# Mamba2 decay matrices from cumulated decays spread through a DRAM scratch, and the residual scaling in the HGRN stage

## The chip, the cores and the metric

One core of one Trainium2 chip runs the whole program in one launch. The time is device time in microseconds, the median of several runs. Its engines are TensorE (PE, with its weight loads PEld), VectorE (DVE), ScalarE (ACT), GpSimd (POOL) and SyncE (SP, which issues the weight loads). Each runs its own instruction list in order and waits for the others by semaphores.

## The reference

Two transformer-like blocks on 512 tokens of width 1024, in float32. The second puts 16 learned tokens in front (528 in all) and feeds two mixers from one projection: HGRN2 (8 heads) and Mamba2 (16 heads in 2 groups), whose outputs are projected back together and added to the residual. The part that matters here, cut from the Mamba2 mixer:

```python
da = dt * a                                   # a < 0: one decay per token and head
a_cum = jnp.cumsum(ac, axis=2)                # within a chunk
seg = a_cum[:, :, :, None] - a_cum[:, :, None, :]
l_mat = jnp.exp(jnp.where(causal[:, :, None, None], seg, -jnp.inf))
cb = jnp.einsum('bnigs,bnjgs->bnijg', cc, bc)
y_diag = jnp.einsum('bnijgh,bnjghp->bnighp', cb[..., None] * l_mat, xc)
# per chunk: y_off from the state, state = chunk decay * state + u
```

The residual that enters block 2 is block 1's output, normalised and scaled: each token's row is multiplied by one factor.

## The kernel before

Activations lie feature by token. Every large product is a `gemm`: for each of 8 k-tiles the weight is split into a rounded high part `wh` (ACT, line 82) and a rest `wl` (DVE, line 83), and three passes (`pass3`) add `XH*wh`, `XL*wh` and `XH*wl` into PSUM tiles `acc`. In block 2 the 528 tokens make two segments of 264, so one k-tile is six products. The weights of a gemm are split two gemms ahead.

All smaller work hangs between the k-tiles. A `Lane` holds generators; each `tick` after a k-tile counts a lane down, and each `yield n` asks for n ticks. This fixes where PE's small products stand among the projection products; the other engines' lists are put in order by the framework that records the program, which can bring a later instruction ahead of an earlier one on an engine.

Block 2's first stage projects the Mamba2 inputs. `m2_conv` makes each 128-feature tile: DVE scales `acc` by `R` into `mu`, ACT starts the convolution `mc`, DVE adds three taps, ACT makes the tanh into `mu`, DVE the last step; `to_tokens` transposes `mc` on PE into `xtm` (token by feature). `m2_tables` computes `dt`, `da` and, on PE with the triangle `le`, the cumulated decays and totals.

`m2_core` runs once per group, over five chunks: the 16 learned tokens and four of 128. For a chunk it needs, per head, the decay matrix. Before, that is made thus (lines 850 to 882): POOL multiplies the triangle `le` by `da`, split in a high and a low part, into tiles `sr` of 128 by 4 heads by 128; PE multiplies these by the strict triangle `gtr`, which sums the decays between two tokens into PSUM; ACT takes the exponential into `Lm`; DVE multiplies by the masked scores `cbm`; PE multiplies with `xdt`. Beside it PE makes the state's products (`S` with `mC`, `xde` with `btm`), DVE updates `S` and `yt`, and POOL multiplies `xtm` by the skip weight and adds `yt`. `prepare(c + 1)` runs during chunk c. Group 0's chunks stand among the last Mamba2 input projections, group 1's among those of the gate `z`.

`resid` multiplies the eight tiles of `H` by the token factor `R1`. Before, it is added to lane 2 as the decay tables begin, one multiply per six ticks. The HGRN stage (`hg_head`, `hg_back`, `gate`) follows, and only then `w_out` adds to `H`.

Of the kernel before, what the change touches and what calls it, by code (L numbers as in the profile page):

```python
# [126 lines left out]
class Builder:  # L127
    def __init__(self, ctx, tc, ins, out):
        self.tc, self.nc, self.ins, self.out = tc, tc.nc, ins, out
        nc = self.nc  # L130
        self.const = ctx.enter_context(tc.tile_pool(reuse_waits="tile", name="const", bufs=1))
        self.wraw = ctx.enter_context(tc.tile_pool(reuse_waits="tile", name="wraw", bufs=2))
        self.whl = ctx.enter_context(tc.tile_pool(reuse_waits="tile", name="whl", bufs=3))
        self.stat = ctx.enter_context(tc.tile_pool(reuse_waits="tile", name="stat", bufs=1))
        self.acc_p = ctx.enter_context(tc.tile_pool(reuse_waits="tile", name="accp", bufs=4, space=PSUM))
        self.sm_p = ctx.enter_context(tc.tile_pool(reuse_waits="tile", name="smp", bufs=4, space=PSUM))
        self.W = WStream(nc, ins["wts"], self.wraw, self.whl)
        self.lanes = [Lane() for _ in range(3)]
        self.hold = False
        self.pend = []  # L140

# [162 lines left out]
    def setup(self):  # L304
        nc, c = self.nc, self.const
        self.H = c.tile([P, KD, L], F32, name="H")
        self.XH = c.tile([P, KD, L], F32R, name="XH")
        self.XL = c.tile([P, KD, L], F32R, name="XL")
        self.par_t = c.tile([P, NPAR], F32, name="par_t")
        cm = c.tile([P, 4 * P + 16], F32, name="cm")  # L310
        self.four = cm[:, 4 * P:]
        self.ident, self.le, self.gt, self.ones = (cm[:, i * P:(i + 1) * P] for i in range(4))
        nc.scalar.preload_act_table_set("exp_and_others")
        nc.sync.dma_start(out=self.H[:, 0, META:L], in_=self.ins["xT"][:, 0])
        nc.scalar.dma_start(out=self.par_t[:, 0:8], in_=self.ins["par"][:, 0:8])
        self.W.load_to(0)
        for k in range(1, KD):
            nc.sync.dma_start(out=self.H[:, k, META:L], in_=self.ins["xT"][:, k])
            if k == 2:
                self.W.load_to(1)  # L320
        nc.gpsimd.dma_start(out=self.par_t[:, 8:NPAR], in_=self.ins["par"][:, 8:NPAR])
        nc.gpsimd.dma_start(out=cm, in_=self.ins["cm"])
        nc.gpsimd.dma_start(out=self.H[:, :, 0:META], in_=self.ins["metaT"])
# [434 lines left out]
    def m2_tables(self, mp, dtp):  # L758
# [31 lines left out]
        self.ts(a, a, -1.0, ALU.mult)  # L790
        self.da = w("da")
        self.mul(self.da, self.dt, bc(a))
        self.dah, self.dal = (mp.tile([P, 5, 16], F32R, name=f"da{i}") for i in "hl")
        self.gtr = mp.tile([P, P], F32R, name="gtr")
        nc.scalar.copy(self.gtr, self.gt)
        self.split(self.dah, self.dal, self.da)
        yield 12
        ps = self.sm()
        self.mm(ps[:, 16:80], self.le, self.da[:, 1:5, :])
# [5 lines left out]
        self.ei, self.cd, self.dte = w("ei"), w("cd"), w("dte")  # L805
        self.act(f2(self.ei), cum, AF.Exp)
        self.act(f2(self.cd), tot, AF.Exp)
        nc.vector.tensor_copy(f2(v), cum)
        self.sub(f2(self.dte), tot, f2(v))
        self.act(self.dte, self.dte, AF.Exp)  # L810
        self.mul(self.dte, self.dte, self.dt)
        yield 2

    def m2_conv(self, mp, accs, segs, R, j):
# [24 lines left out]
    def m2_core(self, mp, g, C, btm, cbm, xtm):  # L839
# [6 lines left out]
        def prepare(c):  # L846
            n = dims[c][0]
            x = xtm[0:n, c, 512 * g:512 * g + 512]
            b64 = lambda t: t[0:n, c, hs].unsqueeze(2).to_broadcast([n, 8, 64])
            srs, xde = [], None  # L850
            for hh in range(2):
                h0 = 8 * g + 4 * hh
                sr = []
                for i, da in enumerate((self.dah, self.dal)):
                    t = mp.tile([P, 4, P], F32R, tag=f"sr{i}", name="sr", bufs=2)
                    da = da[0:n, c, h0:h0 + 4].bitcast(F32).unsqueeze(2).to_broadcast([n, 4, n])
                    nc.gpsimd.tensor_tensor(out=t[0:n, :, 0:n], in1=da, op=ALU.mult,
                                            in0=self.le[0:n, 0:n].unsqueeze(1).to_broadcast([n, 4, n]))
                    sr.append(t)
                srs.append(sr)  # L860
            xdt = mp.tile([P, 512], F32, tag="xdt", name="xdt", bufs=2)
            self.mul(h3(xdt[0:n]), h3(x), b64(self.dt))
            if c < 4:
                xde = mp.tile([P, 512], F32, tag="xde", name="xde", bufs=1)
                self.mul(h3(xde[0:n]), h3(x), b64(self.dte))
            return srs, xdt, xde
        nxt = prepare(0)
        yield 4
        for c in range(5):
            n, tok = dims[c]  # L870
            srs, xdt, xde = nxt
            x = xtm[0:n, c, 512 * g:512 * g + 512]
            b64 = lambda t: t[0:n, c, hs].unsqueeze(2).to_broadcast([n, 8, 64])
            Ls = []
            for hh in range(2):
                ps = self.sm()
                p3 = ps[:, 0:4 * n].rearrange("p (h i) -> p h i", i=n)
                for i, t in enumerate(srs[hh]):
                    self.mm(p3[0:n], self.gtr[0:n, 0:n], t[0:n, :, 0:n], start=i == 0, stop=i == 1)
                Lm = mp.tile([P, 4, P], F32, tag="Lm", name="Lm", bufs=2)  # L880
                self.act(Lm[0:n, :, 0:n], p3[0:n], AF.Exp)
                Ls.append(Lm)
            if c:
                po = self.sm()
                self.mm(po[0:n], C[:, tok], S)
# [3 lines left out]
            md = self.par("m2d", 8 * g, 8)[0:n].unsqueeze(2).to_broadcast([n, 8, 64])  # L889
            nc.gpsimd.tensor_tensor(out=h3(x), in0=h3(x), in1=md, op=ALU.mult)  # L890
            yield 2
            for hh in range(2):
                self.mul(Ls[hh][0:n, :, 0:n], Ls[hh][0:n, :, 0:n], cbm[0:n, c, 0:n].unsqueeze(1).to_broadcast([n, 4, n]))
            if c:
                t = mp.tile([P, 512], F32, tag="yt", name="yt", bufs=1)
                self.mul(h3(t[0:n]), h3(po[0:n]), b64(self.ei))
# [7 lines left out]
            yield 5  # L904
            pd = self.sm()
            for h in range(8):
                self.mm(pd[0:n, 64 * h:64 * h + 64], Ls[h // 4][0:n, h % 4, 0:n], xdt[0:n, 64 * h:64 * h + 64])
            yield 1
            if c == 0:
                self.add(x, pd[0:n], x)  # L910
# [153 lines left out]
    def block2(self, sqh, sqg):  # L1064
        nc, tc, st = self.nc, self.tc, self.stat
        H, XH, XL = self.H, self.XH, self.XL
        W2 = T + 2
        R, R1 = self.r_tile(), self.r_tile()

        def norm2():  # L1070
            s1 = self.tok_sums(self.blocks(sqh))
            s2 = self.tok_sums(self.blocks(sqg))
            x, y, t = (st.tile([P, 8], F32, name="q" + i) for i in "xyt")
            r1, r3 = y[:, 0:4], y[:, 4:8]

            self.ts(x[:, 0:4], s1[:, 0:4], 1.0 / D, ALU.mult, EPS, ALU.add)
            self.ts(t[:, 0:4], x[:, 0:4], EPS, ALU.mult)
            self.stt(x[:, 4:8], s2[:, 0:4], 1.0 / D, t[:, 0:4], ALU.mult, ALU.add)
            self.rsqrt(x, y, t)
            yield 6  # L1080
            self.spread([r3[:, b:b + 1] for b in range(4)], R, META)
            nc.vector.tensor_copy(R[:, 0:META], self.rmeta)
            self.spread([r1[:, b:b + 1] for b in range(4)], R1, META)

        def resid():
            for k in range(KD):
                self.mul(H[:, k, META:L], H[:, k, META:L], R1[:, META:L])
                yield 6
# [6 lines left out]
        with ExitStack() as sy:  # L1095
# [26 lines left out]
            with tc.tile_pool(reuse_waits="tile", name="m2", bufs=1) as mp:  # L1122
                xtm = mp.tile([P, 5, D], F32, name="xtm")
                nc.gpsimd.memset(xtm[:, 0, :], 0.0)
                Cs = [mp.tile([P, L], F32, name=f"mC{g}") for g in range(2)]
                btms = [mp.tile([P, 5, P], F32, name=f"btm{g}") for g in range(2)]
                cbms = [mp.tile([P, 5, P], F32, name=f"cbm{g}") for g in range(2)]
                self.core_done = [False, False]
# [45 lines left out]
                proj_bc(0)  # L1174
                dtp = mp.tile([P, L + 3], F32, tag="mu", name="dtp", bufs=2)[:, 0:L]
                self.gemm16(wdt, self.par("norm1", 0, KD), segs, 4, lambda a: self.ev_r(dtp, a, segs, R))
                self.lanes[2].add(resid())
                self.lanes[0].add(self.m2_tables(mp, dtp))
                for j in range(4):
                    proj_x(j)  # L1180
# [84 lines left out]
            with tc.tile_pool(reuse_waits="tile", name="hp", bufs=1) as hp:  # L1265
# [31 lines left out]
                for h in range(8):  # L1297
                    if h:
# [14 lines left out]
                    if h > 1:  # L1313
                        gate(h - 1)
                gate(7)
                sqa = st.tile([P, L], F32, tag="sqa", name="sqa", bufs=2)

                def ev_o(m):
# [87 lines left out]
def np_consts():  # L1406
    i = np.arange(P)
    ident = np.eye(P)
    le = (i[:, None] <= i[None, :])
    gt = (i[:, None] > i[None, :])  # L1410
    cm = np.concatenate([ident, le, gt, np.ones((P, P)), i[:, None] % 32 == i[:16]], 1).astype(np.float32)
    dist = P + i[:, None] - np.arange(256)[None, :]
    dist = np.where((dist >= 0) & (dist < P), dist, 1e30).astype(np.float32)
    r64 = np.broadcast_to((np.arange(T) % 64 != 0), (P, T)).astype(np.float32)
# [10 lines left out]
def host_inputs(a, rec):  # L1425
# [41 lines left out]


IN_SHAPES = {
    "xT": (P, KD, T), "metaT": (P, KD, META), "par": (P, NPAR), "cm": (P, 4 * P + 16), "dist": (P, 256),  # L1470
    "r64": (P, T), "r32": (P, PADL), "r4": (P, 17), "wal": (P, T), "wts": (NCH, P, 1024), "wga": (P, KD, 32), "wdt": (P, KD, 32),
}

# [22 lines left out]
```

## Time and profile before

| | |
|---|---|
| median of 3 runs (lowest to highest) | 1801.13 us (1800.87 to 1802.17) |
| the profiled execution's own time | 1800.79 us |
| its span in the trace | 1799.0 us |
| PE, PEld, DVE, ACT, POOL busy | 98%, 86%, 62%, 39%, 10% of the span |
| mean granted clock of TensorE | 0.993 |
| DMA, mean | 85 GB/s |

A busy share counts instructions that run, whatever their speed: a product at the lower clock is busy for longer. PEclk in the windows shows it, 1.00 being 2.4 GHz. Matmul records overlap, so the price of a product is read from the distance of two starts. A releaser in brackets is the instruction whose end let a waiting engine go on.

### The profile page before, as it was taken

Reading aid. Unit: us, or ns where it says so; the run is one execution under the profiler, and the core shown is the slowest. Engines: PE = TensorE matmul, PEld = TensorE weight load, DVE = VectorE, ACT = ScalarE, POOL = GpSimd, SP = SyncE. Lnnn points to the kernel's source line nnn. Section 1 sums busy time; section 2 is a strip of 40 time slices with the busy share of each in tenths; the row PEclk is TensorE's granted clock in tenths of the full one; section 3 lists DMA queues with packets and bytes.
Section 4 is the critical chain, followed back from the end, with each engine's and each line's share of the span. In section 5 each row is a group of like instructions: output and inputs, shape, how many; then the busy total and the mean of one; then the engine's idle time right before and its main releaser. Section 6 shows DMA issues by size and latency. Waiting matters only on the chain. (4 is left out here: it accounts for less than half of the span.)

```text
span 1799.0 us, 26982 instructions
## 1 busy us (share of the span) xinstructions
PE 1767.2 (98%) x11036; PEld 1550.6 (86%) x11036; DVE 1116.0 (62%) x1942; ACT 703.6 (39%) x1097; POOL 174.6 (10%) x226
## 2 busy tenths in 40 slices
PE   8999999999999999999998999999999999999997
PEld 6777778888888888888887989999999999999775
DVE  5476764444467777633698798676743577776332
ACT  5355442222344444333442335545432344444221
POOL 2000000000110000011135451000001000000000
PEclk9999999999999999999998999999999999999998
DMA  5222223333333333333221212222223332333321
GB/s 183 83 71 59 71 82 94 94 94 94 94 94 94 94 94 94 94 94 95 85 71 36 60 48 80 69 82 61 83 74 92 94 88 90 94 94 94 94 84 68
DMA packets 43452, 153.50 MB, mean 85 GB/s; under 512 B 5024, under 2 KB 5168, under 8 KB 43328
## 3 DMA queue, kind: packets, MB, share of 16 engines
q1 hardware_dynamic: 42480, 149.83, 27.4%
q8 instruction: 87, 1.43, 0.3%
q0 software_dynamic: 560, 1.67, 0.3%
q14 instruction: 37, 0.30, 0.1%
q10 hardware_dynamic: 288, 0.27, 0.0%
HBM read 149.66 MB, written 2.10 MB: 84 GB/s over the span
## 5 line engine op out<-in xcount | busy, mean ns | idle before, releaser
L179 PE MATMUL acc<-XH,wh 128*128 128x512 f32 (+3 forms) x2320 | 635.5, 328 | 0.0
L179 PE MATMUL acc<-XH,wl 128*128 128x512 f32 (+3 forms) x2320 | 621.2, 321 | 0.0
L179 PE MATMUL acc<-XL,wh 128*128 128x512 f32 (+3 forms) x2320 | 620.5, 321 | 0.0
L82 ACT CAST wh<-wraw 128x1024 fp32r<-128x1024 f32 (+1 forms) x279 | 291.8, 1046 | 528.3 <-PE acc L179 467.0
L83 DVE TENSOR_TENSOR wl<-wraw,wh 128x1024 fp32r<-128x1024 f32 (+1 forms) x279 | 343.6, 1232 | 214.4 <-ACT wh L82 207.0
L179 PEld LDWEIGHTS acc<-XH,wh 128*128 128x128 f32 x2320 | 385.9, 189 | 43.9 <-issue 8.5
L179 PEld LDWEIGHTS acc<-XH,wl 128*128 128x128 f32 x2320 | 385.8, 189 | 35.4 <-issue 1.5
L179 PEld LDWEIGHTS acc<-XL,wh 128*128 128x128 f32 x2320 | 386.7, 189 | 33.7 <-issue 0.5
L179 PE MATMUL acc<-FH,wh 128*128 128x512 f32 x352 | 140.6, 399 | 0.0
L179 PE MATMUL acc<-FH,wl 128*128 128x512 f32 x352 | 139.0, 395 | 0.0
L179 PE MATMUL acc<-FL,wh 128*128 128x512 f32 x352 | 138.3, 393 | 0.0
L162 DVE SCALAR_TENSOR_TENSOR c<-u,par_t,c 128x512 f32<-128x512 f32 x176 | 131.8, 749 | 6.8 <-ACT c L176 3.7
L150 DVE TENSOR_TENSOR u<-acc,R 128x512 f32<-128x512 f32 (+2 forms) x132 | 63.8, 510 | 90.1 <-PE acc L179 87.0
L334 POOL TENSOR_TENSOR sqa<-sqa,sqt 128x512 f32<-128x512 f32 x27 | 40.9, 1516 | 744.1 <-ACT sqt L176 744.1
L179 PEld LDWEIGHTS acc<-FH,wl 128*128 128x128 f32 x352 | 66.1, 188 | 16.8
L179 PEld LDWEIGHTS acc<-FL,wh 128*128 128x128 f32 x352 | 66.1, 188 | 15.4
L179 PEld LDWEIGHTS acc<-FH,wh 128*128 128x128 f32 x352 | 66.1, 188 | 15.1
L176 ACT ACTIVATE FH<-c 128x512 fp32r<-128x512 f32 x44 | 27.8, 632 | 116.3 <-DVE c L150 116.3
L150 DVE TENSOR_TENSOR H<-H,acc 128x512 f32<-128x512 f32 (+2 forms) x41 | 22.6, 569 | 77.8 <-PE acc L179 77.8
L176 ACT ACTIVATE c<-u,par_t 128x512 f32<-128x512 f32 x88 | 67.8, 770 | 2.6 <-DVE u L150 2.4
L176 ACT ACTIVATE c<-c 128x512 f32<-128x512 f32 x44 | 27.8, 632 | 85.3 <-DVE c L162 85.2
L179 PE MATMUL acc<-yh,wh 128*128 128x256 f32 (+1 forms) x256 | 51.5, 283 | 0.1
(391 smaller groups left out, 2058.5 us busy)
## 6 DMA issues: line engine op xcount, KB each, us to landing
wraw<-in_wts SPq DMA_DIRECT2D x277, 512.0 KB, 3.6
H<-in_xT SPq DMA_DIRECT2D x8, 256.0 KB, 9.5
out<-H SPq DMA_DIRECT2D x7, 256.0 KB, 2.7
wraw<-in_wts SPq DMA_DIRECT2D x2, 256.0 KB, 4.0
r<-in_r POOLq DMA_DIRECT2D x1, 272.0 KB, 4.2
cm<-in_cm POOLq DMA_DIRECT2D x1, 264.0 KB, 5.3
par_t<-in_par POOLq DMA_DIRECT2D x1, 256.0 KB, 4.3
r<-in_r POOLq DMA_DIRECT2D x1, 256.0 KB, 6.6
```

Source lines behind the costliest of these rows:

```text
L82: self.nc.scalar.copy(h[:, e], t[:, e])
L83: self.nc.vector.tensor_tensor(out=l[:, e], in0=t[:, e], in1=h[:, e].bitcast(F32), op=ALU.subtract)
L150: self.nc.vector.tensor_tensor(out=out, in0=a, in1=b, op=op)
L162: self.nc.vector.scalar_tensor_tensor(out=out, in0=a, scalar=s, in1=b, op0=op0, op1=op1)
L176: self.nc.scalar.activation(out=out, in_=a, func=func, scale=scale, **kw)
L179: self.nc.tensor.matmul(out, lhsT, rhs, start=start, stop=stop)
L334: self.nc.gpsimd.tensor_tensor(out=acc, in0=acc, in1=t, op=ALU.add)
```

## The change

The decay matrix is now made from differences of cumulated decays. `m2_tables` keeps the cumulated decays per token (`cum`), has PE make them once more as rows, 16 heads by 128 tokens for each chunk, ACT copies them to `ct`, and a DMA on POOL's queue writes them to a DRAM tile `cumd`. `prepare` no longer has POOL multiply: a DMA on POOL's queue reads eight rows of one chunk and spreads them over all 128 partitions, into a tile `seg` of 128 by 8 heads by 128 (512 KB, two buffers). ACT forms exp(-relu(cum_j - cum_i)) with one Relu per head, whose bias is the head's column of `cum`, and one Exp over all; DVE masks in one multiply. `gt`, `gtr`, `dah`, `dal` and `sr` go. `resid` makes its `R1` itself and runs in a fourth lane that starts at HGRN head 1 and is emptied after the last gate.

```diff
-        self.lanes = [Lane() for _ in range(3)]
+        self.lanes = [Lane() for _ in range(4)]
...
-        self.dah, self.dal = (mp.tile([P, 5, 16], F32R, name=f"da{i}") for i in "hl")
-        self.gtr = mp.tile([P, P], F32R, name="gtr")
-        nc.scalar.copy(self.gtr, self.gt)
-        self.split(self.dah, self.dal, self.da)
...
+        self.cum = v
+        ct = mp.tile([P, 8, P], F32, tag="seg", name="ct", bufs=2)
+        ps, ps0 = self.sm(), self.sm()
+        for c in range(4):
+            self.mm(ps[0:16, c * P:(c + 1) * P], self.da[:, c + 1, :], self.le)
+        self.mm(ps0[0:16, 0:P], self.da[0:16, 0, :], self.le[0:16, :])
+        nc.scalar.copy(ct[0:16, 1:5, :], ps[0:16].rearrange("p (a b) -> p a b", a=4))
+        nc.scalar.copy(ct[0:16, 0, :], ps0[0:16, 0:P])
+        nc.gpsimd.dma_start(out=self.cumd.rearrange("c h t -> h c t"), in_=ct[0:16, 0:5, :])
...
-                    nc.gpsimd.tensor_tensor(out=t[0:n, :, 0:n], in1=da, op=ALU.mult,
-                                            in0=self.le[0:n, 0:n].unsqueeze(1).to_broadcast([n, 4, n]))
+            seg, xde = mp.tile([P, 8, P], F32, tag="seg", name="seg", bufs=2), None
+            nc.gpsimd.dma_start(out=seg, in_=self.cumd[c, hs, :].unsqueeze(0).to_broadcast([P, 8, P]))
...
-                for i, t in enumerate(srs[hh]):
-                    self.mm(p3[0:n], self.gtr[0:n, 0:n], t[0:n, :, 0:n], start=i == 0, stop=i == 1)
-                Lm = mp.tile([P, 4, P], F32, tag="Lm", name="Lm", bufs=2)
-                self.act(Lm[0:n, :, 0:n], p3[0:n], AF.Exp)
-                Ls.append(Lm)
+            Lm = seg[0:n, :, 0:n]
+            for h in range(8):
+                self.act(Lm[:, h, :], Lm[:, h, :], AF.Relu, scale=-1.0, bias=self.cum[0:n, c, 8 * g + h:8 * g + h + 1])
+            self.act(Lm, Lm, AF.Exp, scale=-1.0)
...
-            for hh in range(2):
-                self.mul(Ls[hh][0:n, :, 0:n], Ls[hh][0:n, :, 0:n], cbm[0:n, c, 0:n].unsqueeze(1).to_broadcast([n, 4, n]))
+            self.mul(Lm, Lm, cbm[0:n, c, 0:n].unsqueeze(1).to_broadcast([n, 8, n]))
...
         def resid():
+            R1 = self.r_tile()
+            self.spread([self.r1[:, b:b + 1] for b in range(4)], R1, META)
+            yield 8
...
-                self.lanes[2].add(resid())
...
+                    if h == 1:
+                        self.lanes[3].add(resid(), 4)
...
+                self.flush(3)
```

Three places show what moved in the engines' lists. On PE, in the middle of a chunk (the second of group 0, before):

```order
L179 MATMUL acc<-XH,wl 128x264 x2
L179 MATMUL sm<-sr,gtr 128x512 x4
L179 MATMUL sm<-S_6946,mC_6296 128x512
L179 MATMUL sm<-xde,btm_6298 128x512
L179 MATMUL acc<-XH,wh 128x264 x2
```

and after:

```order
L179 MATMUL acc<-XH,wl 128x264 x2
L179 MATMUL sm<-S_6940,mC_6295 128x512
L179 MATMUL sm<-xde,btm_6300 128x512
L179 MATMUL acc<-XH,wh 128x264 x2
L179 MATMUL acc<-XL,wh 128x264 x2
```

The four triangle products are gone, the state's products stand where they stood. On POOL, the first chunks of group 0 before (`sr`: the triangle times the decays; `xtm` times `par_t`: the skip multiply):

```order
L857 TENSOR_TENSOR sr<-cm,dah 128x512
L857 TENSOR_TENSOR sr<-cm,dal 128x512
L857 TENSOR_TENSOR sr<-cm,dah 128x512
L857 TENSOR_TENSOR sr<-cm,dal 128x512
L890 TENSOR_TENSOR xtm<-xtm,par_t 16x512
L890 TENSOR_TENSOR xtm<-xtm,par_t 128x512
L818 MEMSET mu 128x3
L857 TENSOR_TENSOR sr<-cm,dah 128x512
```

and after:

```order
L816 DMA cumd<-ct 16x5x128
L823 MEMSET mu 128x3
L856 DMA seg<-cumd 128x1024
L881 TENSOR_TENSOR xtm<-xtm,par_t 16x512
L856 DMA seg<-cumd 128x1024
L881 TENSOR_TENSOR xtm<-xtm,par_t 128x512
L823 MEMSET mu 128x3
L856 DMA seg<-cumd 128x1024
```

The multiplies became one DMA issue per chunk, which stand in line with the skip multiplies and the clearing of `mu`. On ACT, at the last chunk of group 0, before (`mu<-mc` is the tanh of a convolution, `wh` a weight cast, `Lm_7333` and `Lm_7338` belong to the chunk before the last):

```order
L176 ACTIVATE Lm_7333<-sm_7330 128x512
L176 ACTIVATE Lm_7338<-sm_7335 128x512
L833 COPY xtm_6294<-sm_7345 128x4x128
L176 ACTIVATE mc_7283<-mu_7282,m2cws_6258 128x528
L836 COPY xtm_6294<-sm_7351 16x128
L82 CAST wh_7422<-wraw_7299 128x1024
L176 ACTIVATE mu_7282<-mc_7283 128x528
L833 COPY xtm_6294<-sm_7382 128x4x128
```

and after:

```order
L838 COPY xtm_6293<-sm_7307 128x4x128
L176 ACTIVATE mc_7246<-mu_7245,m2cws_6257 128x528
L841 COPY xtm_6293<-sm_7313 16x128
L176 ACTIVATE seg_7333<-seg_7333,dv_6625 128x128 x8
L82 CAST wh_7377<-wraw_7262 128x1024
L176 ACTIVATE seg_7333<-seg_7333 128x1024
L176 ACTIVATE mu_7245<-mc_7246 128x528
L838 COPY xtm_6293<-sm_7337 128x4x128
```

The decay work of the last chunk came to stand between the start of that convolution and its tanh; before, its two exponentials came behind the tanh (below the rows shown).

## Rows read from the trace of the kernel before

**Rows 1.** The page, part 1: busy us (share of the span) and instructions of each engine
```profile
PE 1767.2 (98%) x11036; PEld 1550.6 (86%) x11036; DVE 1116.0 (62%) x1942; ACT 703.6 (39%) x1097; POOL 174.6 (10%) x226
```

**Rows 2.** PE's waits, 880 to 1100 us: total us, times, longest
```profile
PE sm L182 <- DVE mc L162: 3.6, 1, 3.6
PE sm L179 <- DVE yt L150: 3.0, 2, 2.5
PE sm L179 <- DVE xde L150: 1.5, 1, 1.5
PE sm L182 <- POOL xtm L913: 1.1, 1, 1.1
```

**Rows 3.** Windows: us; busy PE, PEld, DVE, ACT, POOL; PEclk, DMA share, GB/s
```profile
920.00:940.00 20.00, 18.48 (x136) 16.64 (x134) 18.79 (x35) 8.20 (x18) 12.39 (x11) 0.91 0.18 53
940.00:960.00 20.00, 17.54 (x105) 14.27 (x103) 20.00 (x22) 5.50 (x9) 15.74 (x13) 0.91 0.18 54
980.00:1000.00 20.00, 20.00 (x137) 18.66 (x136) 13.46 (x19) 7.65 (x13) 4.32 (x6) 0.84 0.15 49
1100.00:1150.00 50.00, 49.57 (x468) 49.02 (x467) 41.08 (x125) 26.45 (x60) 2.57 (x11) 1.00 0.23 73
```

**Rows 4.** PE's timeline round one stop: start us, us [idle before <-releaser]
```profile
950.93 0.41 PE L179 MATMUL acc<-XH,wl 128*128 128x264 f32 x2
951.17 1.08 PE L179 MATMUL sm<-sr,gtr 128*128 128x512 f32 x4
952.09 1.02 PE L179 MATMUL sm<-S,mC 128*128 128x512 f32 x2
955.57 1.97 PE L179 MATMUL sm<-xde,btm 128*128 128x512 f32 x2 [2.46 <-DVE yt L150]
957.78 0.64 PE L179 MATMUL acc<-XL,wh 128*128 128x264 f32 x2
```

**Rows 5.** The tile `sr`: duration ns min/median/max, first and last start us
```profile
L857 POOL TENSOR_TENSOR sr<-cm,dah x20: 282/1482/2231, 926.2 to 1051.3; 128x512 fp32r<-128x512 f32 x16, 16x64 fp32r<-16x64 f32 x4
```

**Rows 6.** DVE's groups by form, 928 to 998 us: busy us, mean ns, idle
```profile
L162 DVE SCALAR_TENSOR_TENSOR mc<-mu,m2cws,mc 128x528 f32<-128x528 f32 x18 | 17.9, 996 | 2.0 <-ACT mc L176 1.9
L150 DVE TENSOR_TENSOR Lm<-Lm,cbm 128x512 f32<-128x512 f32 x8 | 12.2, 1538 | 0.2 <-ACT Lm L176 0.2
```

**Rows 7.** The tile `R`: the residual multiplies
```profile
L150 DVE TENSOR_TENSOR H<-H,R x8: 683/684/691, 890.5 to 928.0; 128x512 f32<-128x512 f32 x8
```

**Rows 8.** DVE's timeline, one convolution step with POOL idle
```profile
908.06 0.76 DVE L162 SCALAR_TENSOR_TENSOR mc<-mu,m2cws,mc 128x528 f32<-128x528 f32 x1
```

**Rows 9.** PE's groups by form, 880 to 1100 us: busy us, mean ns, idle
```profile
L179 PE MATMUL sm<-sr,gtr 128*128 128x512 f32 x32 | 9.7, 428 | 0.0
L179 PE MATMUL sm<-sr,gtr 16*16 16x64 f32 x8 | 0.7, 194 | 0.0
```

**Rows 10.** PE's timeline at the cumulated sums
```profile
925.95 1.41 PE L179 MATMUL sm<-da,cm 128*128 128x64 f32 x8
```

**Rows 11.** DVE's timeline ahead of the first gate multiply
```profile
1126.29 0.70 DVE L150 TENSOR_TENSOR hg<-hg,hoT 128x514 f32<-128x514 f32 x1 [2.02 <-ACT hoT L176]
```

**Rows 12.** ACT's groups by form, whole span
```profile
L82 ACT CAST wh<-wraw 128x1024 fp32r<-128x1024 f32 x277 | 290.6, 1049 | 527.8 <-PE acc L179 467.0 <-issue 56.7 <-DMA wraw<-in_wts 2.0
L176 ACT ACTIVATE hon<-sm 128x128 f32<-128x128 f32 x40 | 10.5, 274 | 6.9 <-PE sm L179 6.9
```

**Rows 13.** DMA issues: queue, count, KB each, median us from issue to landing
```profile
wraw<-in_wts SPq DMA_DIRECT2D x277, 512.0 KB, 3.6
r<-in_r POOLq DMA_DIRECT2D x1, 272.0 KB, 4.2
wal<-in_wal POOLq DMA_DIRECT2D x1, 256.0 KB, 7.6
r<-in_r POOLq DMA_DIRECT2D x1, 8.5 KB, 3.8
```

**Rows 14.** PE's timeline at the longest stop
```profile
979.14 0.87 PE L182 MATMUL sm<-cm,mc 128*128 128x128 f32 x5 [3.55 <-DVE mc L162]
```

More of the change, by code (lines that the diff above doesn't have):

```diff
@@ L309, in setup @@
         self.par_t = c.tile([P, NPAR], F32, name="par_t")
-        cm = c.tile([P, 4 * P + 16], F32, name="cm")
-        self.four = cm[:, 4 * P:]
-        self.ident, self.le, self.gt, self.ones = (cm[:, i * P:(i + 1) * P] for i in range(4))
+        cm = c.tile([P, 3 * P + 16], F32, name="cm")
+        self.four = cm[:, 3 * P:]
+        self.ident, self.le, self.ones = (cm[:, i * P:(i + 1) * P] for i in range(3))
         nc.scalar.preload_act_table_set("exp_and_others")
@@ L849, in prepare @@
             b64 = lambda t: t[0:n, c, hs].unsqueeze(2).to_broadcast([n, 8, 64])
-            srs, xde = [], None
-            for hh in range(2):
[L852 to L856, printed above, removed]
-                    nc.gpsimd.tensor_tensor(out=t[0:n, :, 0:n], in1=da, op=ALU.mult,
-                                            in0=self.le[0:n, 0:n].unsqueeze(1).to_broadcast([n, 4, n]))
-                    sr.append(t)
-                srs.append(sr)
+            seg, xde = mp.tile([P, 8, P], F32, tag="seg", name="seg", bufs=2), None
+            nc.gpsimd.dma_start(out=seg, in_=self.cumd[c, hs, :].unsqueeze(0).to_broadcast([P, 8, P]))
             xdt = mp.tile([P, 512], F32, tag="xdt", name="xdt", bufs=2)
@@ L865, in prepare @@
                 self.mul(h3(xde[0:n]), h3(x), b64(self.dte))
-            return srs, xdt, xde
+            return seg, xdt, xde
         nxt = prepare(0)
@@ L870, in m2_core @@
             n, tok = dims[c]
-            srs, xdt, xde = nxt
+            seg, xdt, xde = nxt
             x = xtm[0:n, c, 512 * g:512 * g + 512]
             b64 = lambda t: t[0:n, c, hs].unsqueeze(2).to_broadcast([n, 8, 64])
[L874 to L877, printed above, removed]
-                for i, t in enumerate(srs[hh]):
-                    self.mm(p3[0:n], self.gtr[0:n, 0:n], t[0:n, :, 0:n], start=i == 0, stop=i == 1)
-                Lm = mp.tile([P, 4, P], F32, tag="Lm", name="Lm", bufs=2)
-                self.act(Lm[0:n, :, 0:n], p3[0:n], AF.Exp)
-                Ls.append(Lm)
+            Lm = seg[0:n, :, 0:n]
+            for h in range(8):
+                self.act(Lm[:, h, :], Lm[:, h, :], AF.Relu, scale=-1.0, bias=self.cum[0:n, c, 8 * g + h:8 * g + h + 1])
+            self.act(Lm, Lm, AF.Exp, scale=-1.0)
             if c:
@@ L891, in m2_core @@
             yield 2
-            for hh in range(2):
-                self.mul(Ls[hh][0:n, :, 0:n], Ls[hh][0:n, :, 0:n], cbm[0:n, c, 0:n].unsqueeze(1).to_broadcast([n, 4, n]))
+            self.mul(Lm, Lm, cbm[0:n, c, 0:n].unsqueeze(1).to_broadcast([n, 8, n]))
             if c:
@@ L906, in m2_core @@
             for h in range(8):
-                self.mm(pd[0:n, 64 * h:64 * h + 64], Ls[h // 4][0:n, h % 4, 0:n], xdt[0:n, 64 * h:64 * h + 64])
+                self.mm(pd[0:n, 64 * h:64 * h + 64], Lm[:, h, :], xdt[0:n, 64 * h:64 * h + 64])
             yield 1
@@ L1067, in block2 @@
         W2 = T + 2
-        R, R1 = self.r_tile(), self.r_tile()
+        R = self.r_tile()
         def norm2():
@@ L1082, in norm2 @@
             nc.vector.tensor_copy(R[:, 0:META], self.rmeta)
-            self.spread([r1[:, b:b + 1] for b in range(4)], R1, META)
+            self.r1 = r1
         def resid():
+            R1 = self.r_tile()
+            self.spread([self.r1[:, b:b + 1] for b in range(4)], R1, META)
+            yield 8
             for k in range(KD):
@@ L1125, in block2 @@
                 Cs = [mp.tile([P, L], F32, name=f"mC{g}") for g in range(2)]
+                dp = sy.enter_context(tc.tile_pool(reuse_waits="tile", name="dp", bufs=1, space=bass.MemoryType.DRAM))
+                self.cumd = dp.tile([5, 16, P], F32, name="cumd")
                 btms = [mp.tile([P, 5, P], F32, name=f"btm{g}") for g in range(2)]
@@ L1409, in np_consts @@
     le = (i[:, None] <= i[None, :])
-    gt = (i[:, None] > i[None, :])
-    cm = np.concatenate([ident, le, gt, np.ones((P, P)), i[:, None] % 32 == i[:16]], 1).astype(np.float32)
+    cm = np.concatenate([ident, le, np.ones((P, P)), i[:, None] % 32 == i[:16]], 1).astype(np.float32)
     dist = P + i[:, None] - np.arange(256)[None, :]
@@ L1469 @@
 IN_SHAPES = {
-    "xT": (P, KD, T), "metaT": (P, KD, META), "par": (P, NPAR), "cm": (P, 4 * P + 16), "dist": (P, 256),
+    "xT": (P, KD, T), "metaT": (P, KD, META), "par": (P, NPAR), "cm": (P, 3 * P + 16), "dist": (P, 256),
     "r64": (P, T), "r32": (P, PADL), "r4": (P, 17), "wal": (P, T), "wts": (NCH, P, 1024), "wga": (P, KD, 32), "wdt": (P, KD, 32),
```

## The prediction

> **What bounds the kernel now.** I read the page's busy times first: TensorE (PE) is busy 1767.2 of 1799.0 us [rows 1], so time falls only where PE gets less to do, waits less, or runs at a higher clock. Second, PE's waits in the stretch that the change touches (880 to 1100 us): 3.6 + 3.0 + 1.5 + 1.1 = 9.2 us, three of the four on VectorE (DVE) and one on GpSimd (POOL) [rows 2]. Third, that stretch in 20 us windows. DVE is busy 18.79 and 20.00 of 20 us while PE loses time, so DVE is the engine that is late here; and the granted clock falls to 0.91, 0.91 and 0.84 [rows 3]. Fourth, the timeline of one stop shows how the two belong together: PE waits 2.46 us for `yt`, and two projection products then take 0.64 us where they took 0.41 (they run at the lower of the clock's two levels, 1.2 GHz) until the clock is back [rows 4]. The clock's loss is 20 x (0.09 + 0.09 + 0.16) = 6.8 us over the three stops of 1.5 us and more, about 2.3 us for each.
>
> Why DVE is late: POOL makes 40 `sr` products, 1.48 us each at the median, in this stretch [rows 5]. Beside them DVE slows. From 928 to 998 us the 8 `Lm` multiplies take 1.54 us each and 18 convolution steps 1.00 us [rows 6]; a multiply of the same shape takes 0.684 us with POOL idle [rows 7], such a step alone 0.76 us [rows 8]. That is 8 x 0.854 + 18 x 0.236 = 11.1 us of DVE time.
>
> **The change part by part.**
>
> *PE, removed.* The triangle products: four of 512 columns start 0.92 us before the next product [rows 4]. The 32 full ones [rows 9] are eight such fours, 7.4 us; the 8 small ones are 0.7 us [rows 9]. Together 8.1 us, all on the bounding engine.
>
> *PE, added.* Five exact products that put the cumulated decays into 16 rows, two records each. The nearest row is the existing products with the same `da`, 1.41 us for 8 records [rows 10]: 10 x 0.176 = 1.8 us at most; 0.9 us if they cost half. I take 1.8. The products that spread the residual's scale move and cost the same.
>
> *DVE.* With no `sr` products the 11.1 us mostly go; POOL keeps its skip multiplies and final adds. The 8 residual multiplies of 0.684 us, 5.5 us, leave the stretch too [rows 7]. That is 16.6 us off an engine whose lateness cost PE 9.2 us. So I let all four old stops go, 9.2 us, and their clock loss, 6.8 us. The `dal` split goes, the merged `Lm` multiply is as wide as two before: no change.
>
> *Residual in the HGRN stage.* DVE is busy 41.08 of 50 us there, PE 49.57 [rows 3]. The order puts five of the eight behind one another, just ahead of the gate multiply; today DVE idles 2.02 us at that place [rows 11]. If nothing else hid them, PE would lose 5.5 - 2.0 = 3.5 us; nothing excludes zero, and since the next things that PE needs from DVE are a gemm later, I take 0.
>
> *ScalarE (ACT).* A full chunk gets 8 Relus of 128x128 and one Exp of 1024 columns: 8 x 0.27 + 1.05 = 3.2 us by the nearest rows [rows 12], for two Exps of 512 before. ACT is busy 5.5 of 20 us there [rows 3]. By itself this costs nothing; what it delays does (below).
>
> *POOL and the DMA queues.* Ten spreads of 512 KB replace the products; the DMA share is 0.18 [rows 3], so there is room. The trace shows no such transfer. POOL's loads land in 3.8 us (8.5 KB), 4.2 (272 KB) and 7.6 (256 KB, at the start beside other loads); SyncE's 512 KB in 3.6 [rows 13]. So 3.6 is the lower end and 7.6 the upper. I take 5.0: the 4.2 of the row nearest in place, plus 0.8 for 240 KB more, since SyncE's row allows at most 1.7 for these.
>
> Each spread is a wait for ACT, and behind it on ACT stand weight casts, tanhs and PSUM copies. The casts run two gemms ahead (2 x 48 products x 0.12 = 11.5 us), so they survive. Two other places do not obviously:
>
> Place one, the first chunk. In the new order, from the end of the new products, PE has 81 projection products (0.122 each: two start 0.24 us before the next record [rows 4]), two sets of transposes (0.5 each, half of the 0.87 at the lower clock [rows 14]) and one `xde` product (0.9: 1.02 for the like product of [rows 4] less the overlap that the `sr` four show there) before it needs the masked matrix: 9.9 + 1.0 + 0.9 = 11.8 us. The chain beside it: ACT copies the table out (1.4, five widths of [rows 12]), it lands in DRAM (3.8, the small POOL row), POOL multiplies the skip (1.5), the second spread lands (5.0; ACT's order puts chunk 1's first Relu ahead of chunk 0's Exp, so it is the second that counts), Exp and mask 0.5: 12.2 us. PE waits about 0.5 us; 0 at the lower end, 3.0 at the upper.
>
> Place two, the last chunk of group 0. In ACT's order its 8 Relus, a cast and the Exp now stand ahead of the tanh of the convolution whose transposes PE needs next, the place of today's longest stop, 3.55 us [rows 14]. From the end of chunk 2's products, which free the buffer: DVE still has to make chunk 3's `xde` (1.5, an estimate from two multiplies of 0.684), POOL multiplies 1.5, landing 5.0, Relus 2.2, cast and Exp 2.1, tanh and last step 1.5 (two widths of 528, 0.76 each): 13.8 us. PE has 70 projection products, two 512-wide products and transposes: 8.5 + 1.8 + 0.5 = 10.8. PE waits 3.0 us; 1.6 to 5.6 with the landing. With it goes a dip of the clock, 2.3 us. The next transposes stand behind a Relu likewise, at 0 us with 5.0 and 2.6 with 7.6.
>
> *Sum.* -8.1 + 1.8 - 9.2 - 6.8 + 0.5 + 3.0 + 2.3 = -16.5 us. The profiled execution took 1800.79 us (span 1799.0), the median of the runs is 1801.13. So 1784.3 on that execution and 1784.6 beside the median.
>
> A rule that speaks against the change: the Trainium skill, SBUF — State Buffer, section "SBUF: two separate sides", says that a DMA issued from GpSimd has its descriptors written by GpSimd, which a DVE instruction in a two-port mode shuts out of SBUF, so that the transfer waits for DVE. No run here shows this; the long landings of POOL's loads at the start would agree. By the rule the kernel would take rival one's time, by the row nearest in place the forecast's.
>
> **The rivals.**
>
> *One: the spreads land late.* While DVE works without pause, every spread takes the 7.6 us of POOL's slowest row [rows 13]. Then the first chunk costs 3.0 us, place two 5.6 and the transposes behind it 2.6, each with 2.3 us of clock: 18.1 us instead of 5.8, and the kernel takes 1796.9. For it: group 0's spreads fall where DVE is busy 18.79 and 20.00 of 20 us. Against: 7.6 was met at the start, beside other loads, and the 272 KB load at the end of this stretch landed in 4.2.
>
> *Two: DVE stays late.* POOL's remaining multiplies and adds, about 20 of the size of an `sr` product, still sit beside DVE, which has conv steps, masks and states in each chunk. The stops stay as they are and only PE's net 6.3 us are won: 1794.8. Against: 16.6 us less DVE work set against 9.2 us of stops.
>
> *Three, the other side: the chain is longer than the chunks.* A spread may start only when the products of two chunks before have freed its buffer. From there to the masked matrix: POOL 3.0, landing, Relus, Exp, cast and tanh 5.5, mask 1.3, some 1.2 of queueing: landing + 11. PE covers at most two chunks less one set of products: 2 x (48 x 0.122 + 1.8 + 2.8) - 2.8 = 18.1 us (16 records at 0.176 for the set). The four pairs of full chunks lose 4 x (landing - 7.1 + 2.3). This equals the 22.3 us gained at a landing of 10.4; at 12, should it be slow that all partitions read one small DRAM region, the loss is 28.8 and the kernel takes 1807.6. Against: no row is above 7.6 at this size.
>
> **How the numbers follow.** Forecast 0.62, rival one 0.17, two 0.11, three 0.10. What this kernel's measurement can tell from no change is about 0.2%, 3.6 us. The forecast's own range is 1777 (all stops gone, the new products at half price: 1801.1 - 22.3 - 0.9 = 1777.9) to 1791. To leave out no more than 2 in 10 the range takes in rivals one and two: 1777 to 1799. Faster needs under 1797.5: the forecast, nine tenths of rivals one and two, 0.87. Within 0.2%: 0.05, from rival one's tail and the near end of three. Slower 0.08, rival three.
>
> **What would show it.** In the profile after: no `sr` rows and PE's count down by 30 records; `Lm` (now `seg`) multiplies near 1.25 us for 1024 columns; the DMA table with ten `seg` loads and their landing (5 us right, 7.6 rival one, over 10 rival three); PE's waits in 880 to 1100 us under 5 us in all, the longest at transposes of `mc`; the granted clock 0.95 or more from 920 to 980 us. In the HGRN stage PE stays above 49 of 50 us. Waits of PE on DVE as long as today's, with short landings, would show rival two. The forecast is wrong if PE waits over 1 us at more than two chunks.

## The result and the profile after

The changed kernel takes 1785.3 us (median of 4 runs, 1784.96 to 1787.46) where the kernel before takes 1801.65 in the same comparison: ratio 0.9912, interval 0.9894 to 0.9929. The forecast was 1784.6. The profiled execution has a span of 1783.1 us where it had 1799.0, and a mean granted clock of 0.998 where it had 0.993.

First the page's busy line, which answers to [rows 1]: PE has 30 records fewer, 40 products less and 10 records more, and POOL 48.6 us less work.

```profile
PE 1754.1 (98%) x11006; PEld 1539.9 (86%) x11006; DVE 1095.1 (61%) x1931; ACT 724.3 (41%) x1167; POOL 126.0 (7%) x197
```

PE's waits in 880 to 1100 us (total us, times, longest), answering to [rows 2]. They come to 5.9 us where they were 9.2, and the longest is 1.8 where it was 3.6. Two stops are longer than 1 us, so the prediction's sign of being wrong, more than two such chunks, did not appear.

```profile
PE sm L182 <- DVE mc L162: 3.3, 3, 1.8
PE sm L182 <- DVE yt L150: 1.0, 1, 1.0
PE sm L179 <- DVE seg L150: 1.0, 1, 1.0
PE sm L179 <- DVE hb L150: 0.4, 1, 0.4
PE sm L179 <- DVE S L150: 0.2, 1, 0.2
```

The windows that answer to [rows 3] (columns as there). The granted clock is 1.00 in all of them; DVE still works 19.86 of 20 us in 940 to 960, but no longer 18.79 in the window before it.

```profile
920.00:940.00 20.00, 18.96 (x148) 16.63 (x147) 13.65 (x25) 10.63 (x31) 6.01 (x8) 1.00 0.32 108
940.00:960.00 20.00, 19.82 (x140) 17.19 (x138) 19.86 (x29) 13.82 (x30) 4.69 (x7) 1.00 0.33 107
980.00:1000.00 20.00, 18.12 (x152) 17.55 (x151) 14.78 (x26) 11.43 (x27) 3.20 (x3) 1.00 0.35 106
1100.00:1150.00 50.00, 49.61 (x469) 49.03 (x468) 39.29 (x103) 24.21 (x54) 2.17 (x10) 1.00 0.22 65
```

PE's timeline at the new products and at three of the stops that are left. The ten new records take 1.36 us. 971.46 is the place two of the prediction; 989.72 is the next set of transposes.

```profile
923.06 1.36 PE L179 MATMUL sm<-cm,da 128*16 128x128 f32 x10
962.01 0.28 PE L182 MATMUL sm<-cm,mc 128*16 128x128 f32 x1 [0.98 <-DVE yt L150]
971.46 0.76 PE L182 MATMUL sm<-cm,mc 128*128 128x128 f32 x5 [1.38 <-DVE mc L162]
989.72 1.28 PE L182 MATMUL sm<-cm,mc 128*128 128x128 f32 x10 [1.78 <-DVE mc L162]
```

The DMA issues (KB each, median us to landing), where [rows 13] had no such transfer: a spread lands in 4.0 us.

```profile
seg<-cumd POOLq DMA_DIRECT2D x10, 512.0 KB, 4.0
cumd<-ct POOLq DMA_DIRECT2D x1, 40.0 KB, 2.0
```

### The profile page after: what moved, and what is told of

The parts are those of the page before. It is cut to its first block, busy times and chain, and to the rows that moved or that the text cites. A ratio compares the mean times of both kernels' runs of the same rounds, so it can differ in the third digit from the quotient of the medians.

```text
span 1783.1 us, 26942 instructions
## 1 busy us (share of the span) xinstructions
PE 1754.1 (98%) x11006; PEld 1539.9 (86%) x11006; DVE 1095.1 (61%) x1931; ACT 724.3 (41%) x1167; POOL 126.0 (7%) x197
```

## The experiments

My theory was that two parts paid: POOL's multiplies, which hold VectorE up, and the triangle products on TensorE. The rivals were that the residual's move did it (A), that the products stood in time that TensorE would have waited anyway (B), and that POOL's multiplies harm nobody (D, E). In these comparisons the kernel before took 1801.0 to 1802.1 us.

**The residual put back** (the move undone):

```
+                self.lanes[2].add(resid())
...
-                    if h == 1:
-                        self.lanes[3].add(resid(), 4)
```

> The changed kernel with the residual scaling (eight multiplies H by R1 of about 0.68 us and the spread of R1) put back into the Mamba2 stage; decay matrices stay as in the changed kernel. Theory (the stops of TensorE went because POOL's triangle multiplies no longer slow VectorE, and the triangle products left TensorE): VectorE gets some 5.5 us of work back in the first group's chunks but is not slowed, so 1 to 4 us come back: 1786 to 1789 us, with at most one stop over 2 us in 920 to 1000. Rival A (the stops went because the residual scaling left the stage): the 9.2 us of stops and most of the 6.8 us of clock loss come back: 1795 to 1800 us.

1786.69 us, ratio to before 0.9915 (0.9902 to 0.9929): 1.4 us above the changed kernel, less than can be told from nothing. The waits come to 7.0 us, with one long stop at the first chunk (PE's timeline):

```profile
944.18 1.06 PE L179 MATMUL sm<-xdt,seg 16*16 16x64 f32 x16 [3.89 <-DVE seg L150]
```

The residual's multiplies on DVE do not make it: DVE stands idle for 4.89 us just before. In this order of POOL's list a skip multiply of 4.00 us stood ahead of the first spreads, and ACT waited for their landing (POOL's timeline, then ACT's):

```profile
932.55 4.00 POOL L881 TENSOR_TENSOR xtm<-xtm,par_t 16x512 f32<-16x512 f32 x1 [2.29 <-DVE xde L150]
936.50 1.12 POOL L856 DMA_DIRECT2D seg<-cumd  x2
```

```profile
940.72 1.69 ACT L176 ACTIVATE seg<-seg,dv 16x16 f32<-16x16 f32 x8 [3.78 <-DMA seg<-cumd]
```

**Only the residual moved**, in the kernel before (the same edit the other way round):

> The kernel before with the residual scaling alone moved to the HGRN stage; triangle multiplies on POOL and products on TensorE stay. Theory: POOL still slows VectorE, so the stops and the lower clock mostly stay: 1 to 5 us faster than before, 1796 to 1800 us. Rival A (the residual scaling was the cause of the stops): 9 to 14 us faster, 1787 to 1792 us, the granted clock in 920 to 1000 back at 1.00.

1802.62 us, ratio 1.0004 (0.9995 to 1.0013). Here I missed: not 1 to 5 us, nothing. The two long stops are there and have grown a little (2.75 us for 2.46, 3.98 for 3.55); the stop of 1.51 us for `xde` is gone, and one of 1.29 us for POOL's `sr` has come. PE's waits in 880 to 1100 us come to 10.2 us, of which these are the first two lines. Rival A falls by both runs.

```profile
PE sm L182 <- DVE mc L162: 4.1, 2, 4.0
PE sm L179 <- DVE yt L150: 3.5, 3, 2.8
```

**The products back on TensorE**, in the changed kernel:

```
+                for i in range(2):
+                    self.mm(p3[0:n], self.gtr[0:n, 0:n], self.src[0:n, :, 0:n], start=i == 0, stop=i == 1)
```

> The changed kernel with the 40 triangle products put back on TensorE at their old place, on constant tiles that are ready long before, so they wait for nobody; their outputs are read by nobody. It prices the removed products alone. Theory: each costs its step of about 0.23 us (32 large) or less (8 small), 8.1 us in all, since TensorE runs without a gap there: 1792 to 1794 us. Rival B (the products stood in time in which TensorE would have waited anyway, 5.9 us of waits being left in the stage): 0 to 3 us, 1785 to 1788 us.

1795.19 us (five runs, 1791.5 to 1796.65), 9.9 us more, a little above the 1794 that I allowed. The profiled execution, at the changed kernel's mean granted clock of 0.998, has 7.2 us more span, its PE 7.9 us more work (1762.0); the three executions above 1795 us have a clock of 0.994 to 0.996. With DVE relieved the products cost about their time.

**POOL's multiplies back**, in the changed kernel:

```
+                for i in range(2):
+                    nc.gpsimd.tensor_tensor(out=t[0:n, :, 0:n], in1=da, op=ALU.mult,
+                                            in0=self.le[0:n, 0:n].unsqueeze(1).to_broadcast([n, 4, n]))
...
+                self.mm(px[0:16, 0:16], t[0:n, 0, 0:16], t[0:n, 1, 0:16])
```

> The changed kernel with POOL's 40 triangle multiplies put back, each pair of a chunk behind the issue of that chunk's spread; their only reader is one 16x16 product per tile, 20 in all and under 2 us together. It prices the multiplies on POOL alone: they slow VectorE beside them and hold up POOL's queue, which issues the spreads. Theory: 4 to 10 us come back as stops of TensorE behind VectorE, 1789 to 1795 us, with VectorE's mask multiply and mc group slower than the 1436 and 855 ns of the changed kernel. Rival A (residual scaling was the cause) and rival D (POOL's multiplies cost nobody anything): 0 to 2 us, which are the 20 small products: 1785 to 1787 us.

1803.34 us, ratio 1.0006 (0.9997 to 1.0015): the whole gain and more is gone, 18 us where I expected 4 to 10. From 928 to 998 us DVE's convolution steps take 1130 ns where the changed kernel has 855, its masks 1759 where it has 1436. The 20 small products are under 1 us of it, by the distance of starts (a pair starts 0.05 us before the next product, or 0.13 at the lower clock). Put back one at a time, the two parts cost 9.9 + 18.0 = 27.9 us, though both together were worth 16.3, and the new parts cost only some 5 us (below). But here the multiplies also stand in the queue that issues the spreads, which they did not in the kernel before, and how much of the 18 us that is, the run does not tell. That called for taking the two parts out of the kernel before one at a time.

**The products alone taken out:**

```
-                    self.mm(p3[0:n], self.gtr[0:n, 0:n], t[0:n, :, 0:n], start=i == 0, stop=i == 1)
-                self.act(Lm[0:n, :, 0:n], p3[0:n], AF.Exp)
+                self.act(Lm[0:n, :, 0:n], srs[hh][1][0:n, :, 0:n].bitcast(F32), AF.Exp)
```

> The kernel before without the 40 triangle products: ScalarE's exponent reads the tile that POOL multiplied, so the decays are not summed; POOL's multiplies and the residual scaling stay. It takes the products alone away. Additive theory (the prediction's sum): 8.1 us faster, 1793 us, since TensorE goes on with the next product at once. Rival B (as the run with POOL's multiplies put back now suggests: with POOL multiplying, VectorE sets the pace of the stage, and the time of the products comes back as waits for VectorE): 0 to 3 us faster, 1798 to 1801 us, with the stops behind VectorE in 880 to 1100 grown from 9.2 to 13 us or more.

1803.09 us, ratio 1.0011 (1.0003 to 1.0020): not 8 us faster but 2.1 slower. PE's busy time fell by 7.1 us (1760.1), and its waits rose from 9.2 to 18.4:

```profile
PE sm L179 <- DVE xde L150: 8.8, 1, 8.8
PE sm L179 <- DVE S L150: 4.3, 2, 2.4
PE sm L179 <- DVE sny L162: 3.5, 1, 3.5
PE sm L182 <- DVE mc L162: 1.8, 2, 1.2
```

The stop of 8.8 us reads on in DVE's timeline: two multiplies on 16 rows take 8.45 us, while POOL (its timeline below) runs one `sr` multiply after another from 926 to 943 us, four of them in 4.02 us.

```profile
930.86 8.45 DVE L150 TENSOR_TENSOR xdt<-xtm,dt 16x512 f32<-16x512 f32 x2
```

```profile
931.14 4.02 POOL L857 TENSOR_TENSOR sr<-cm,dah 128x512 fp32r<-128x512 f32 x4
```

In the kernel before, POOL's first large `sr` multiply starts only at 929.36, when PE's products have freed a buffer. Without the products it starts earlier and does not pause, so this edit takes the products away and makes POOL's run denser as well. The 2.1 us hold both.

**The multiplies alone taken out:**

```
-                    nc.gpsimd.tensor_tensor(out=t[0:n, :, 0:n], in1=da, op=ALU.mult,
...
+                srs.append((self.src, self.src))
```

> The kernel before without POOL's 40 triangle multiplies: the products run at their old place on one constant tile, so the decays are those of a constant; the residual scaling stays. It takes the multiplies alone away. Additive theory: the stops of 9.2 us and the clock's 6.8 us shrink to about 6 and 0: 8 to 10 us faster, 1791 to 1793 us. Rival B (VectorE's pace decides; with VectorE relieved and the products as filler for TensorE, hardly a stop is left): 10 to 14 us faster, 1787 to 1791 us, with VectorE's 128x512 Lm multiply under 1300 ns where it took 1538. Rival E (VectorE is not slowed by POOL): 0 to 2 us, 1799 to 1801 us.

1785.91 us, ratio 0.9916 (0.9902 to 0.9929): 15.1 us faster with all 40 products still there, more than either expectation. The `Lm` multiply takes 1191 ns, as rival B wanted. The waits are 2.0 us and the clock is 1.00 in each window from 880 to 1100 us:

```profile
PE sm L182 <- DVE mc L162: 1.6, 1, 1.6
PE sm L179 <- DVE hb L150: 0.4, 1, 0.4
```

**Neither** (both edits):

> The kernel before without POOL's triangle multiplies and without the 40 products: the exponent reads one constant tile, so the decays are those of a constant. It is the fourth of the square with before, without products (1803.1 us) and without multiplies (1785.9 us), and stands for the change with its new parts at no cost. If, with VectorE relieved, a product costs its time: 7 to 9 us under the run without multiplies, 1777 to 1779 us, so that the new parts of the changed kernel (spreads, cumulated sums, differences) cost 6 to 8 us. If the products still fill waits: 1783 to 1786 us.

1780.44 us, ratio 0.9882 (0.9867 to 0.9897): 5.5 us under the run without multiplies (6.1 by the two ratios, as the two were measured beside different runs of the kernel before), between the two expectations. PE's busy time falls by 7.4 us (1759.9 to 1752.5), and 2.1 us come back as waits (2.0 to 4.1):

```profile
PE sm L182 <- DVE mc L162: 2.3, 2, 1.6
PE sm L179 <- DVE sny L162: 1.0, 1, 1.0
PE sm L179 <- DVE hb L150: 0.4, 1, 0.4
PE sm L182 <- DVE yt L150: 0.4, 1, 0.4
```

**Why POOL's multiplies harm.** In the kernel before, DVE's timeline and POOL's show it from 942 to 947 us (the last row of each stands some 9 us later):

```profile
942.33 0.94 DVE L162 SCALAR_TENSOR_TENSOR mc<-mu,m2cws,mc 128x528 f32<-128x528 f32 x1
943.20 1.52 DVE L150 TENSOR_TENSOR Lm<-Lm,cbm 128x512 f32<-128x512 f32 x1
944.64 1.54 DVE L162 SCALAR_TENSOR_TENSOR mc<-mu,m2cws,mc 128x528 f32<-128x528 f32 x1
946.11 1.52 DVE L150 TENSOR_TENSOR Lm<-Lm,cbm 128x512 f32<-128x512 f32 x1
954.84 0.67 DVE L150 TENSOR_TENSOR yt<-yt,sm 128x512 f32<-128x512 f32 x1
```

```profile
942.67 1.50 POOL L857 TENSOR_TENSOR sr<-cm,dal 128x512 fp32r<-128x512 f32 x1
944.13 1.48 POOL L857 TENSOR_TENSOR sr<-cm,dah 128x512 fp32r<-128x512 f32 x1
945.58 1.50 POOL L857 TENSOR_TENSOR sr<-cm,dal 128x512 fp32r<-128x512 f32 x1
954.32 1.50 POOL L857 TENSOR_TENSOR sr<-cm,dal 128x512 fp32r<-128x512 f32 x1
```

Both go in steps of about 1.45 us. DVE's operations take 0.68 to 0.76 us alone [rows 7, 8], and POOL's multiply took 1.04 us at 929.36, where it started 0.02 us ahead of a DVE multiply. So they mostly take turns, one each, and overlap little: 1.45 us a pair where the two add up to 1.72 to 1.80. The run without products shows that it need not be one each. DVE's last row has one input in PSUM and keeps 0.67 us in the middle of a multiply of POOL. The Trainium skill, SBUF — State Buffer, section "Who interferes with whom", says that a VectorE instruction with two inputs from SBUF and a GpSimd instruction that reads SBUF exclude each other, not one that only writes. Two runs test turns for reads against other harm. In one, ScalarE makes the tiles; in the other, POOL stays as busy but only writes:

```
+                        self.act(t[0:n, h, 0:n], self.le[0:n, 0:n], AF.Copy, scale=da[0:n, c, h0 + h:h0 + h + 1].bitcast(F32))
```

> The kernel before with the triangle multiplies made by ScalarE, one 128x128 copy scaled by the head's decay each (160 of them in place of 40 on POOL, some 0.3 us each), instead of by POOL; nothing else changes, the result too is that of the kernel before. If the harm of POOL's multiplies was that VectorE and POOL wait for each other (their operations alternate at 1.5 us in the trace of before), most of the 15.1 us go: 1786 to 1792 us. If the harm was that the tiles came late, it stays or grows, as ScalarE takes 4.6 us for a chunk and then the exponents: 1798 to 1806 us.

```
+                    for r in range(2):
+                        nc.gpsimd.memset(t[0:n, :, 0:n].bitcast(F32), -0.01)
```

> The kernel before with each of POOL's 40 triangle multiplies (two inputs from SBUF, 1.04 us where nothing stands beside it) replaced by two memsets of the same tile (0.53 us each, no input), so that POOL is as busy in the same places and TensorE reads the same tiles, which now hold a constant; the decays are those of that constant. If what costs is that POOL's and VectorE's reads of SBUF exclude each other, an engine that only writes does no harm: 1785 to 1788 us, as without the multiplies (1785.9 us), and VectorE's mc group back under 850 ns. If what costs is POOL being busy and the tiles or its other work coming late: 1795 to 1802 us.

On ScalarE: 1787.9 us, ratio 0.9922 (0.9909 to 0.9934), 14.2 us faster, though 160 operations took the place of 40. With memsets: 1785.17 us, ratio 0.9912 (0.9895 to 0.9929), as without multiplies, with POOL busy 10.68 us in 940 to 960 (15.74 before, where each multiply takes longer). There DVE's convolution group from 928 to 998 us (busy, mean ns) is back at 789 ns where [rows 6] has 996, and the memsets keep their 0.52 us:

```profile
L162 DVE SCALAR_TENSOR_TENSOR mc<-mu,m2cws,mc 128x528 f32<-128x528 f32 x18 | 14.2, 789 | 1.8 <-ACT mc L176 1.7
```

```profile
L857 POOL MEMSET sr<- x72: 141/524/541, 929.6 to 1035.8; 128x512 f32 x64, 16x64 f32 x8
```

So it is POOL's reading, not its being busy or its tiles' lateness. The rule and the runs agree.

**What the new parts cost, and a better version.** The changed kernel stands 4.9 us above the one with neither (5.4 by the two ratios). Three runs shorten the way of the spreads: issue by SyncE, issue two chunks ahead into three buffers, and both.

```
-            nc.gpsimd.dma_start(out=seg, in_=self.cumd[c, hs, :].unsqueeze(0).to_broadcast([P, 8, P]))
+            nc.sync.dma_start(out=seg, in_=self.cumd[c, hs, :].unsqueeze(0).to_broadcast([P, 8, P]))
```

> The changed kernel with the ten spreads issued by SyncE, whose queue also carries the weight loads, instead of POOL. If POOL's issues and descriptors cost VectorE something, VectorE's operations get faster and 1 to 3 us go: 1782 to 1784 us. If the spreads queue behind weight loads that wait for a buffer, they land later than 4.0 us and TensorE waits longer: 1787 to 1800 us. If neither: 1785 to 1786 us, which I take.

```
+        segt = [fetch(0), fetch(1)]
...
+            if c < 3:
+                segt.append(fetch(c + 2))
```

> The changed kernel with three buffers for the spreads, each fetched two chunks ahead, so that ScalarE need not wait for a landing (it waited 1.53, 1.05, 0.47 and 2.12 us for four of them). If the chain spread, subtraction, exponent, mask multiply still sets the remaining 5.9 us of TensorE's waits, 2 to 4 us go: 1781 to 1783 us. If VectorE's own load sets them (it is busy 19.86 of 20 us in 940 to 960), nothing: 1784 to 1786 us, which I take.

> The changed kernel with both: the spreads issued by SyncE and fetched two chunks ahead into three buffers. Each alone took 3.5 and 2.0 us. If both gains are the same one (the spreads leave POOL's queue, where they stood behind its multiplies of 1.0 to 2.6 us, and so land earlier), the two together give no more than the first: 1780.5 to 1782.5 us, which I take. If they add: 1779 to 1780.5 us.

By SyncE 1781.77 us (ratio 0.9892, 0.9878 to 0.9905), two ahead 1783.27 (0.9901, 0.9886 to 0.9916), both 1780.55 (0.9881, 0.9868 to 0.9895). I expected the first two to change nothing, so both were misses; the third fell on the edge that I had drawn between the two cases (1780.5). Its gain of 4.8 us lies between the first alone (3.5) and the sum (5.5), and the intervals cannot tell which. With both, the kernel still makes the real decays, is 4.8 us faster than the changed one and equal to the one with neither. The landing does not get shorter (medians: 4.0 us by POOL, 3.7 by SyncE, 4.6 two ahead, 4.3 with both); what goes, at the first chunk at least, is the wait for a place in POOL's queue. ScalarE's timeline of the changed kernel shows it there, and that of the kernel with both 3.45 us earlier at the same step (0.92 us of that at the row above it already):

```profile
931.99 1.69 ACT L176 ACTIVATE seg<-seg,dv 16x16 f32<-16x16 f32 x8
936.80 0.40 ACT L176 ACTIVATE seg<-seg,dv 128x128 f32<-128x128 f32 x1 [3.12 <-issue]
```

```profile
931.07 1.69 ACT L176 ACTIVATE seg<-seg,dv 16x16 f32<-16x16 f32 x8
933.35 0.97 ACT L176 ACTIVATE seg<-seg,dv 128x128 f32<-128x128 f32 x3
```

"Issue" there is the landing of the second spread, which POOL could issue only at 931.79, behind a skip multiply of 2.56 us. The long stop with the residual put back is the same wait, with 4.00 us of skip multiply. In the kernel with both, PE's stops from 920 to 1000 us are down to these two (PE's timeline):

```profile
967.77 0.77 PE L182 MATMUL sm<-cm,mc 128*128 128x128 f32 x5 [1.15 <-DVE mc L162]
984.10 1.28 PE L182 MATMUL sm<-cm,mc 128*128 128x128 f32 x10 [0.45 <-DVE mc L162]
```

## Why the prediction was right, step by step

The sum was -16.5 us, and -16.3 was measured, but by three blocks of which two were mis-sized by 2.6 and 2.7 us in opposite directions. The mechanism was right; that the sum is right to 0.2 us is luck. Between the runs the blocks are -15.1 - 5.5 + 4.9 = -15.7 us.

- *DVE relieved, old stops and clock gone.* Predicted -9.2 - 6.8 = -16.0; the run without multiplies gives -15.1. Its waits fall by 7.2 us, and PE's busy time by 7.3 (1767.2 to 1759.9) though it does the same products, with the clock at 1.00 in every window: that is the clock. Mechanism and size hold. Of DVE's work the prediction took off 11.1 us for POOL's multiplies and 5.5 for the residual. Of the first, 7.0 us went in its stretch (759 ns for 996, 1191 for 1538 in [rows 6]); the second won nothing that can be told, since moving the residual alone left the long stops.
- *The triangle products.* Predicted -8.1. The step "all on the bounding engine" failed as a term by itself: with DVE relieved they were worth 5.5 us, since of the 7.4 us of PE's work 2.1 came back as waits. Taken out of the kernel before they won nothing (+2.1): the waits for DVE grew by 9.2 us. The longest of these, 8.8 us, stands beside POOL's denser run, so what the products alone would win there, with POOL's run as it was, is not shown.
- *The new parts.* Predicted +1.8 + 0.5 + 3.0 + 2.3 = +7.6; measured 4.9 (the changed kernel less the one with neither). The new products took 1.36 us for 1.8. Place one took 0.98 for 0.5, with the second spread landing in the 5.0 us taken for it (931.79 to 936.8). The skip multiply in its chain took 2.56 us for 1.5. Place two took 1.38 for 3.0: ACT waited for that landing, 4.2 us after the issue for the 5.0 taken, but DVE set a weight split of 1.39 us between the tanh and the last step, which the sum had not. The clock's dip of 2.3 did not come. In their place two stops stand that I had at nothing: 1.78 us at the next transposes, which I priced at 0 for a landing of 5.0, though the spread ahead of them landed in 5.1, and 0.98 at 962.01. So waits of 5.9 us are left, where I had written under 5.
- *The residual in the HGRN stage.* Predicted 0; the two runs that move it alone give 1.4 and 1.3 us of opposite sign, neither to be told from nothing, and PE keeps 49.61 of 50 us in 1100 to 1150.

Rival one (late landing) and rival three (chain longer than the chunks) fall with the landing: 4.0 us at the median and 5.1 at most, beside a DVE busy 19.86 of 20 us. The 7.6 us of rival one was not POOL's slowest row (a load of 128 KB took 7.7), nor the slowest at its size (SyncE's 256 KB took 9.5); that changes nothing here. The rule of the Trainium skill quoted in the prediction speaks of VectorE in a two-port mode. No wait of that kind shows in these landings, but no trace tells whether any VectorE instruction beside them was in such a mode, so the rule is not tested here, and giving the kernel rival one's time by it was not justified. Rival two (DVE stays late, the stops stay as they are) falls with PE's waits in the changed kernel and with the run without multiplies. Its argument, that POOL's other operations still stand beside DVE, is true but small: in the changed kernel one mask multiply took 2.31 us, beside POOL's final add (DVE's timeline), where its neighbours took 1.21 to 1.23.

```profile
951.71 2.31 DVE L150 TENSOR_TENSOR seg<-seg,cbm 128x1024 f32<-128x1024 f32 x1
```

## What to carry to other kernels

Work on GpSimd that reads SBUF beside VectorE operations with two inputs from SBUF can double the time of these (0.68 to 0.76 us became 1.5 here); where a stage's pace hangs on VectorE, move that work to ScalarE or a DMA even if it is more work (160 operations on ScalarE for 40 on GpSimd still won 14.2 us). Don't add up savings on two engines as if they were independent: where a stage waits for a late engine, less work on the engine that waits may win nothing until the late one is relieved, so price the parts in that order. Look at what stands ahead of a transfer in the queue that issues it: here a multiply on GpSimd that itself waited for VectorE.

## What the runs showed of the hardware that I had not expected

The granted clock did not follow the length of the short stops. In the kernel before, the stop of 1.51 us before 933.87 stands in a window at 0.91 [rows 2, 3]. In the kernel with the products back on constants, stops of 1.48 and 1.99 us left the clock at 1.00 (PE's timeline, then the windows):

```profile
943.19 1.13 PE L179 MATMUL sm<-xde,btm 128*128 128x512 f32 x2 [1.48 <-DVE xtm L150]
972.15 0.74 PE L182 MATMUL sm<-cm,mc 128*128 128x128 f32 x5 [1.99 <-DVE mc L162]
```

```profile
940.00:960.00 20.00, 18.52 (x127) 15.93 (x125) 18.67 (x28) 13.02 (x30) 4.10 (x7) 1.00 0.30 107
960.00:980.00 20.00, 18.01 (x130) 15.94 (x129) 16.18 (x23) 9.47 (x19) 6.55 (x7) 1.00 0.33 105
980.00:1000.00 20.00, 18.84 (x160) 18.60 (x160) 13.20 (x21) 14.05 (x33) 3.19 (x3) 1.00 0.27 80
```

Products on 16 rows nearby do not decide it. The stop of 1.51 us has four of them 3 us ahead and one right behind; but that of 1.48 us has 16 of them 3 us ahead, and a stop of 1.44 us in the run with POOL's multiplies put back has none near (the last ends 19 us ahead) and stands in a window at 0.83 (1040 to 1060 us; PE's timeline):

```profile
1040.57 2.83 PE L179 MATMUL sm<-xdt,seg 128*128 128x64 f32 x16 [1.44 <-DVE yt L150]
```

So 2.3 us of clock for every stop was too much, and why the dips of the changed kernel stayed out is open.
